# Forget-gate projection units placed between the value projections of a hybrid mixer kernel

## The chip, the cores and the metric

The kernel runs on one core of one Trainium2 chip. The metric is the device time of the program in microseconds (us). The engines are TensorE (PE; its weight loads are listed as PEld), VectorE (DVE), ScalarE (ACT), GpSimd (POOL) and SyncE (SP, which here issues loads); ScalarE also issues DMAs, for the stores.

## The reference, cut to what matters

One layer of a mixer with three kinds of heads over 2048 tokens of width 1024. A modulated RMS norm gives h, one wide projection `p = h @ w_in` is split into thirteen parts, three mixers work on them, and an output projection and a last norm follow.

```
h = rms_norm(x) * (1 + scale) + shift
qa, ka, va, lra, ga, qb, fb, ib, gb, qc, kc, vc, gc = split(h @ w_in)
log_alpha = log_sigmoid(lra @ w_gla_gate2 + b) / 16       # gate of mixer a
log_f = logaddexp(log(lb), log1p(-lb) + log_sigmoid(fb))  # forget gate of mixer b
k_b = (1 - lb) * sigmoid(-fb)
o_a = gated_linear_attn(qa, ka, va, log_alpha)            # 4 heads
o_b = gated_linear_attn(silu(qb), k_b, ib, log_f)         # 4 heads
o_c = stick_breaking_attn(qc, kc, vc)                     # 4 heads
out = rms_norm(x + gate * (concat(gated o_a, o_b, o_c) @ w_out)) * final_norm_w
```

The change concerns the projection to `fb` (256 columns) with the gate's arithmetic behind it, and its place among the projections to `va`, `vc` and `ib`.

## The kernel before, in words

All matmuls of the projections are split in three: high part by high part, high by low, low by high. The split h lies in SBUF as four blocks of 512 tokens (`hT`), taken in the order 3, 2, 1, 0 (`ORDER`).

A unit is one PSUM accumulation. `fm_unit` (lines 149 to 157) gives a 128-column slice of the projection for 512 tokens, columns on partitions, by 24 matmuls of 512 columns; its PSUM tile `acc` comes from `psA`, two buffers. `tm_unit` (159 to 169) gives up to 272 columns for 128 tokens, tokens on partitions, by 24 matmuls of 256 or 272 columns; its PSUM tiles come from `ps1`, four buffers. After each unit an `evac` function takes the result out of PSUM, by a ScalarE copy into a staging tile and a store that ScalarE issues. All staging tiles, of `fm_unit` and of `tm_unit`, have the tag `st` in the pool `stg`, three buffers of 2 KB per partition.

Weights are loaded by `split_w` (135 to 144): SP loads a raw tile (tag `wraw`, two buffers), ScalarE casts the high part (line 141), VectorE subtracts for the low part (line 142). For `fm_unit` they go to the tags `whi` and `wlo` of the pool `wp`, two buffers each; for `tm_unit` to a pool `wv` of its own.

The work around the change, in the order of the text:

- `value_cols` (571 to 575) projects one group of columns for all tokens in 16 `tm_unit`s. It is called for the upper half of `va` with the 16 columns of `lra` (line 629), for `vc` (634), for `ib` (635) and for the lower half of `va` (636).
- The gate of mixer a runs inside the first two of them: `z_units` (599) and `z_out` (609 to 620). `z_out` takes a staging tile `st` and a scratch tile `dz`, which has the tag `whi` or `wlo` of `wp` (line 616).
- Then `st1` is closed, which gives back the value weights, `ps1` and the small tiles, `kp` is opened for the keys and queries of the stick-breaking stream, and the pool `hf` in the same memory behind it.
- The forget gate: two groups of four `fm_unit`s (661 to 664) with `ev_forget` (644 to 659). It copies the PSUM tile to `st` (648), stores it, computes `log_sigmoid` (539 to 544: VectorE, two ScalarE activations, VectorE), `lk = g - st` on GpSimd (653), `bound_decay` (546 to 551: VectorE, two activations, VectorE) and `decay_sums` (523 to 537: a scan and small tiles on VectorE, one activation), stores `bc` to `s_db` (656), computes `lk - bc` on GpSimd (657) and stores it to `s_kb` (658). The tiles `tmp`, `g`, `bc` and `lk` have three buffers each.
- Then the ScalarE table for the sigmoid is loaded (`sig`, line 793), and two streams are interleaved (760 to 777): the stick-breaking attention (`sb_stream`, 680 to 758) and 34 more `fm_unit`s for the features and gates (`fm_stream`, 668 to 678), five of which, the lead units, come first in the text. A step of the stick-breaking stream has two score products (725, 726) into `zt`, a sigmoid (728), a mask on GpSimd (730), a scan of products on VectorE (734), transposes (738), a copy `PT` to SBUF by ScalarE or VectorE (741, 743) and the weighted sums `av` (750). Its loads are `V` and `Dd` (696, 697; combined on VectorE in 698 and 699), `K` (704) and `Q` (709).

The gated linear attention of both mixers, the output projection and the norm follow; they read `s_db`, `s_kb`, `s_ib`, `s_va` and the features back from DRAM.

The order on each engine's queue is fixed when the program is built. Outside the blocks marked as manually ordered, the builder takes what is ready by its own estimate of times, and the text decides between what is ready; so the queues need not follow the text. Tiles take a buffer of their tag when their first instruction is placed.

Of the kernel before, what the change touches and what calls it, by code (L numbers as in the profile page):

```python
# [8 lines left out]
F32 = mybir.dt.float32  # L9
# [9 lines left out]
P = 128  # L19
T = 2048  # L20
# [16 lines left out]
C_QA, C_KA, C_VA, C_LR, C_GA = 0, 256, 512, 1024, 1040  # L37
C_QB, C_FB, C_IB, C_GB = 1552, 1808, 2064, 2320
C_QC, C_KC, C_VC, C_GC = 2576, 2832, 3088, 3344
# [3 lines left out]
def hybrid_mixer_kernel(ctx, tc, x, c, w_ada, b_ada, w_in, w2, bg, gnw, lbl, hnw,  # L43
                        w_out, fnw, masks, sel2, out):
    nc = tc.nc
# [17 lines left out]
    s_vc = dram("s_vc", [T + 1, 256])  # L63
    s_ib = dram("s_ib", [T, 256])
# [124 lines left out]
    def ev_tm(*parts):  # L189
        def f(ps, tt):  # L190
            w = max(b for _, _, b in parts)
            st = stg.tile([P, 272], F32, tag="st", name="stt")
            nc.scalar.copy(st[:, 0:w], ps[:, 0:w])  # L193
            for dst, a, b in parts:
                nc.scalar.dma_start(dst[tt * P:(tt + 1) * P], st[:, a:b])
        return f
# [374 lines left out]
    def value_cols(col0, ncols, step, evac):  # L571
        w = split_w(col0, wv, ncols, step)
        for n in ORDER:
            for u in range(4):
                tm_unit(w, ncols, 4 * n + u, evac)
# [23 lines left out]
    def z_units(n, l4):  # L599
        pt = ps1.tile([96, 512], F32, tag="lr", name="pt", bufs=1)  # L600
        for v in range(4):
            nc.tensor.transpose(pt[:, v * P:(v + 1) * P], l4[:, v, :], ident)
        lrT = vals.tile([96, 512], F32R, tag="lrT", name="lrT")
        nc.vector.tensor_copy(lrT, pt)
        z_ready.extend((n, lrT, j) for j in range(2))
# [16 lines left out]
    def with_z(evac):  # L622
        def f(ps, tt):
            if z_ready:
                z_out(*z_ready.pop(0))
            evac(ps, tt)
        return f

    value_cols(C_VA + 256, 272, 136, with_z(ev_va))
    z_units(*pending.pop(0))  # L630
    vz = vals.tile([1, 256], F32, name="vz")
    nc.vector.memset(vz, 0.0)
    nc.sync.dma_start(s_vc[0:1], vz)
    value_cols(C_VC, 256, 128, with_z(ev_tm((s_vc[1:T + 1], 0, 256))))
    value_cols(C_IB, 256, 128, ev_tm((s_ib, 0, 256)))
    value_cols(C_VA, 256, 128, ev_tm((s_va[:, 0:256], 0, 256)))
    st1.close()

    st2 = ExitStack()
    kp = st2.enter_context(tc.tile_pool(name="kp", bufs=5, reuse_waits="tile"))  # L640
    sth = ExitStack()
    hf = sth.enter_context(tc.tile_pool(name="hf", bufs=3, reuse_waits="tile"))

    def ev_forget(j):
        def f(ps, n):
            nsl = slice(n * 512, (n + 1) * 512)
            st = stg.tile([P, 512], F32, tag="st", name="st")
            nc.scalar.copy(st, ps)
            nc.scalar.dma_start(s_feat["fb"][j][:, nsl], st)
            tmp, g, bc, lk = (hf.tile([P, 512], F32, tag=t, name=t) for t in ("tmp", "g", "bc", "lk"))  # L650
            log_sigmoid(g, st, tmp)

            nc.gpsimd.tensor_tensor(lk, g, st, op=ALU.subtract)
            bound_decay(g, tmp, j)
            decay_sums(2 + j, n, bc, g, 1.0)
            nc.scalar.dma_start(s_feat["db"][j][:, nsl], bc)
            nc.gpsimd.tensor_tensor(lk, lk, bc, op=ALU.subtract)
            nc.scalar.dma_start(s_feat["kb"][j][:, nsl], lk)
        return f

    for j in range(2):
        w = split_w(C_FB + j * P, wp, P, P)
        for n in ORDER:
            fm_unit(w, n, ev_forget(j))
    sth.close()


    def fm_stream(blocks, after):
# [649 lines left out]
```

## Time and profile before

| | |
|---|---|
| time, median of 3 runs | 1297.59 us (1294.85 to 1298.18) |
| the profiled execution's own time | 1294.26 us |
| its span in the trace | 1292.2 us |
| TensorE busy | 1212.9 us, 94% of the span |
| VectorE busy | 742.1 us, 57% |
| ScalarE busy | 471.7 us, 37% |
| GpSimd busy | 162.9 us, 13% |
| mean granted TensorE clock | 0.976 |

The busy time of an engine is the time in which at least one of its instructions runs, so a TensorE that is busy throughout may still be at its lower clock; the granted clock is listed beside it (1.00 is 2.4 GHz, 0.50 is 1.2 GHz). A line of the timeline gives start, duration, engine, source line, operation, output and inputs, and in brackets how long the engine had been idle before and whose instruction released it.

### The profile page before, as it was taken

How to read it: one execution, taken by the hardware profiler on the slowest of the kernel's cores; microseconds unless marked ns; L12 is line 12 of the kernel's file. 1: busy time of each engine (PE TensorE's matmuls, PEld its weight loads, DVE VectorE, ACT ScalarE, POOL GpSimd, SP SyncE). 2: the span in 40 equal slices, each digit the busy share in tenths (PEclk: the TensorE clock that was granted, in tenths of full speed). 3: DMA queues.
4: the chain of work that ended last, by engine and by line, in shares of the span. 5: the costliest groups of instructions: out<-in, count | busy, mean ns of one | idle time of the engine just before them, and what ended most of it. 6: DMA issues, size and time to landing. Idle time of an engine off the chain costs nothing.

```text
span 1292.2 us, 22081 instructions
## 1 busy us (share of the span) xinstructions
PE 1212.9 (94%) x8682; PEld 991.8 (77%) x8682; DVE 742.1 (57%) x1268; ACT 471.7 (37%) x860; POOL 162.9 (13%) x197
## 2 busy tenths in 40 slices
PE   7899999999999789999999999998978897999997
PEld 7777789899998667777777776766867774777775
DVE  4866325700009873535545488877776768765652
ACT  3376423421115342322333244543333434253621
POOL 3210000000003300000000001012432312010000
PEclk8999999999999989999999999998988997999999
DMA  9765442422133341322323323127877657464621
GB/s 265 240 232 180 147 126 91 143 82 86 46 99 112 126 106 54 92 72 86 100 68 86 109 73 92 34 62 238 264 222 208 195 174 241 133 224 132 203 82 51
DMA packets 177566, 173.73 MB, mean 134 GB/s; under 512 B 39625, under 2 KB 131882, under 8 KB 177454
## 3 DMA queue, kind: packets, MB, share of 16 engines
q1 hardware_dynamic: 144970, 128.70, 33.7%
q10 hardware_dynamic: 32484, 43.54, 9.7%
q8 instruction: 70, 1.15, 0.4%
q14 instruction: 42, 0.34, 0.1%
HBM read 113.47 MB, written 58.73 MB: 133 GB/s over the span
## 4 chain that ended last, share of the span: by engine, by line
PE 62%; DVE 13%; DMA 6%; issue 5%; ACT 2%; POOL 1%; SPq 0%; ACTq 0%; POOLq 0%; DVEq 0%
PE av L750 6%; PE acc L154 5%; PE acc L156 5%; PE acc L155 5%; PE acc L166 4%; PE acc L168 4%; PE acc L167 4%; PE pt L738 4%; PE acc L260 4%; PE y L1194 4%; PE y L1192 4%; PE y L1193 4%; DMA kt<-s_kb 2%; DVE W L858 2%; DVE f L734 2%
## 5 line engine op out<-in xcount | busy, mean ns | idle before, releaser
L734 DVE TENSOR_TENSOR_SCAN f<-f 128x512 f32<-128x512 f32 (+3 forms) x160 | 169.9, 1091 | 22.0 <-ACT f L728 11.9
L154 PE MATMUL acc<-hTh,whi 128*128 128x512 f32 x400 | 160.1, 402 | 9.9 <-ACT st L185 4.3
L156 PE MATMUL acc<-hTh,wlo 128*128 128x512 f32 x400 | 157.5, 394 | 0.0
L155 PE MATMUL acc<-hTl,whi 128*128 128x512 f32 x400 | 157.4, 394 | 0.0
L166 PE MATMUL acc<-whi,hTh 128*128 128x256 f32 (+1 forms) x512 | 146.2, 285 | 1.5 <-ACT stt L193 1.5
L168 PE MATMUL acc<-whi,hTl 128*128 128x256 f32 (+1 forms) x512 | 145.8, 285 | 0.0
L167 PE MATMUL acc<-wlo,hTh 128*128 128x256 f32 (+1 forms) x512 | 145.6, 284 | 0.0
L260 PE MATMUL acc<-hTh,whi 128*128 128x512 f32 x240 | 103.8, 432 | 1.7 <-ACT hTh L244 1.7
L260 PE MATMUL acc<-hTl,whi 128*128 128x512 f32 x240 | 97.9, 408 | 4.3 <-DVE hTl L250 4.3
L1192 PE MATMUL y<-wh,hTh 128*128 128x512 f32 x256 | 101.8, 398 | 0.0
L1193 PE MATMUL y<-wl,hTh 128*128 128x512 f32 x256 | 101.6, 397 | 0.0
L728 ACT ACTIVATE f<-zt 128x512 f32<-128x512 f32 (+3 forms) x160 | 82.1, 537 | 52.9 <-DVE f L734 24.7
L1194 PE MATMUL y<-wh,hTl 128*128 128x512 f32 x256 | 100.1, 395 | 0.4 <-DVE hTl L1160 0.4
L166 PEld LDWEIGHTS acc<-whi,hTh 128*128 128x128 f32 x512 | 97.8, 191 | 1.9 <-ACT stt L193 1.7
L154 PEld LDWEIGHTS acc<-hTh,whi 128*128 128x128 f32 x400 | 75.5, 189 | 29.9 <-ACT st L185 5.6
L167 PEld LDWEIGHTS acc<-wlo,hTh 128*128 128x128 f32 x512 | 97.8, 191 | 0.1
L168 PEld LDWEIGHTS acc<-whi,hTl 128*128 128x128 f32 x512 | 97.8, 191 | 0.1
L260 PE MATMUL acc<-hTh,wlo 128*128 128x512 f32 x240 | 97.4, 406 | 0.0
L750 PE MATMUL av<-PT,V 128*64 128x128 f32 x960 | 89.7, 282 | 0.6 <-DVE PT L743 0.6
L156 PEld LDWEIGHTS acc<-hTh,wlo 128*128 128x128 f32 x400 | 75.3, 188 | 17.0 <-issue 1.4
L738 PE MATMUL pt<-ident,f 128*128 128x128 f32 x544 | 87.0, 283 | 0.9 <-DVE f L734 0.7
L155 PEld LDWEIGHTS acc<-hTl,whi 128*128 128x128 f32 x400 | 75.6, 189 | 15.2 <-issue 1.0
(206 smaller groups left out, 2106.8 us busy)
## 6 DMA issues: line engine op xcount, KB each, us to landing
wraw<-in_w_in_dram SPq DMA_DIRECT2D x36, 512.0 KB, 4.9
xt<-in_x_dram SPq DMA_DIRECT2D x16, 512.0 KB, 5.2
wa<-in_w_ada_dram SPq DMA_DIRECT2D x16, 512.0 KB, 5.6
Q<-s_qc SPq DMA_DIRECT2D x64, 128.0 KB, 3.1
ot<-s_o SPq DMA_DIRECT2D x32, 256.0 KB, 3.4
gt<-s_gate SPq DMA_DIRECT2D x32, 256.0 KB, 4.2
r<-in_x_dram SPq DMA_DIRECT2D x16, 512.0 KB, 5.6
out_dram<-r SPq DMA_DIRECT2D x15, 512.0 KB, 2.7
```

The costliest lines, as they stand in the source:

```text
L154: mm(ps, hi[:, k, :], th[:, k, :], start=(k == 0), stop=False)
L155: mm(ps, hi[:, k, :], tl[:, k, :], start=False, stop=False)
L156: mm(ps, lo[:, k, :], th[:, k, :], start=False, stop=(k == KT - 1))
L166: mm(o, th[:, k, s], hi[:, k, 0:ncols], start=(k == 0), stop=False)
L167: mm(o, th[:, k, s], lo[:, k, 0:ncols], start=False, stop=False)
L168: mm(o, tl[:, k, s], hi[:, k, 0:ncols], start=False, stop=(k == KT - 1))
L260: mm(ps, a[:, k, :], b[:, k, :], start=(k == 0 and i == 0), stop=(k == KT - 1 and i == 2))
L734: nc.vector.tensor_tensor_scan(fr, fr, fr, carry[u], op0=ALU.mult, op1=ALU.bypass)
L750: last[0] = mm(av[u * 64:(u + 1) * 64, :], (Dd if diag else V)[J][:, b, :], PT[:, b, :], start=diag, stop=(J == 0 and b == 0))
L1192: mm(y, oh[:, k, us], wh, start=(k == 0), stop=False)
L1193: mm(y, oh[:, k, us], wl, start=False, stop=False)
L1194: mm(y, ol[:, k, us], wh, start=False, stop=(k == KT - 1))
```

## The change

The pool `hf` is opened inside `st1`, with two buffers of `tmp`, `g` and `bc` and one of `lk`. The loop over the two groups of forget units becomes a function `forget_gate(j)`. Group 0 is called between the projections to `vc` and `ib`, group 1 between `ib` and the lower half of `va`. `ev_forget` computes the same. The DMA scratch that is set aside in SBUF at the start of the program is set to 1024 bytes per partition in place of the default, so that all pools fit.

```diff
--- before.py
+++ after.py
@@ -626,20 +626,7 @@
             evac(ps, tt)
         return f
 
-    value_cols(C_VA + 256, 272, 136, with_z(ev_va))
-    z_units(*pending.pop(0))
-    vz = vals.tile([1, 256], F32, name="vz")
-    nc.vector.memset(vz, 0.0)
-    nc.sync.dma_start(s_vc[0:1], vz)
-    value_cols(C_VC, 256, 128, with_z(ev_tm((s_vc[1:T + 1], 0, 256))))
-    value_cols(C_IB, 256, 128, ev_tm((s_ib, 0, 256)))
-    value_cols(C_VA, 256, 128, ev_tm((s_va[:, 0:256], 0, 256)))
-    st1.close()
-
-    st2 = ExitStack()
-    kp = st2.enter_context(tc.tile_pool(name="kp", bufs=5, reuse_waits="tile"))
-    sth = ExitStack()
-    hf = sth.enter_context(tc.tile_pool(name="hf", bufs=3, reuse_waits="tile"))
+    hf = st1.enter_context(tc.tile_pool(name="hf", bufs=2, reuse_waits="tile"))
 
     def ev_forget(j):
         def f(ps, n):
@@ -647,7 +634,8 @@
             st = stg.tile([P, 512], F32, tag="st", name="st")
             nc.scalar.copy(st, ps)
             nc.scalar.dma_start(s_feat["fb"][j][:, nsl], st)
-            tmp, g, bc, lk = (hf.tile([P, 512], F32, tag=t, name=t) for t in ("tmp", "g", "bc", "lk"))
+            tmp, g, bc, lk = (hf.tile([P, 512], F32, tag=t, name=t, bufs=2 - (t == "lk"))
+                              for t in ("tmp", "g", "bc", "lk"))
             log_sigmoid(g, st, tmp)
 
             nc.gpsimd.tensor_tensor(lk, g, st, op=ALU.subtract)
@@ -658,11 +646,25 @@
             nc.scalar.dma_start(s_feat["kb"][j][:, nsl], lk)
         return f
 
-    for j in range(2):
+    def forget_gate(j):
         w = split_w(C_FB + j * P, wp, P, P)
         for n in ORDER:
             fm_unit(w, n, ev_forget(j))
-    sth.close()
+
+    value_cols(C_VA + 256, 272, 136, with_z(ev_va))
+    z_units(*pending.pop(0))
+    vz = vals.tile([1, 256], F32, name="vz")
+    nc.vector.memset(vz, 0.0)
+    nc.sync.dma_start(s_vc[0:1], vz)
+    value_cols(C_VC, 256, 128, with_z(ev_tm((s_vc[1:T + 1], 0, 256))))
+    forget_gate(0)
+    value_cols(C_IB, 256, 128, ev_tm((s_ib, 0, 256)))
+    forget_gate(1)
+    value_cols(C_VA, 256, 128, ev_tm((s_va[:, 0:256], 0, 256)))
+    st1.close()
+
+    st2 = ExitStack()
+    kp = st2.enter_context(tc.tile_pool(name="kp", bufs=5, reuse_waits="tile"))
 
 
     def fm_stream(blocks, after):
@@ -1300,7 +1302,8 @@
     from concourse import mybir as _mybir
     from concourse.bass_utils import run_bass_kernel_spmd as _run
 
-    nc = _bacc.Bacc("TRN2", target_bir_lowering=False, num_devices=1)
+    nc = _bacc.Bacc("TRN2", target_bir_lowering=False, num_devices=1,
+                    dynamic_dma_scratch_size=1024)
     arrays, args = {}, []
     consts = {'masks': _masks(), 'sel2': _selectors()}
     for name in _INS + list(consts):
```

## Rows read from the trace of the kernel before

**Rows 1.** Page, busy time: us, share of the span and instructions of each engine.

```profile
PE 1212.9 (94%) x8682; PEld 991.8 (77%) x8682; DVE 742.1 (57%) x1268; ACT 471.7 (37%) x860; POOL 162.9 (13%) x197
```

**Rows 2.** Windows: length, busy us and instructions per engine, PEclk, DMA share, GB/s.

```profile
260.00:280.00 20.00, 20.00 (x169) 20.00 (x169) 0.00 (x0) 2.61 (x7) 0.00 (x0) 1.00 0.14 47
375.27:450.00 74.73, 67.13 (x287) 53.97 (x286) 59.40 (x95) 30.80 (x53) 25.12 (x16) 0.98 0.37 125
375.27:467.70 92.43, 79.72 (x352) 63.93 (x350) 70.65 (x112) 38.42 (x66) 25.88 (x18) 0.97 0.42 133
440.00:450.00 10.00, 7.49 (x28) 5.73 (x27) 7.92 (x18) 2.15 (x4) 2.59 (x2) 0.83 0.28 105
465.79:482.80 17.01, 17.01 (x120) 12.54 (x120) 14.58 (x16) 6.82 (x15) 0.59 (x2) 0.83 0.11 34
```

**Rows 3.** Timeline of VectorE, its first instruction of the forget gate.

```profile
381.56 0.69 DVE L541 SCALAR_TENSOR_TENSOR tmp<-st 128x512 f32<-128x512 f32 x1 [87.26 <-ACT st L648]
```

**Rows 4.** Timeline of TensorE, three of its six gaps from 375 to 467.

```profile
421.85 0.50 PE L154 MATMUL acc<-hTh,whi 128*128 128x512 f32 x1 [2.33 <-ACT st L648]
...
444.80 0.79 PE L154 MATMUL acc<-hTh,whi 128*128 128x512 f32 x1 [2.51 <-ACT st L185]
...
465.79 0.69 PE L750 MATMUL av<-PT,Dd 128*64 128x128 f32 x4 [4.38 <-DVE PT L743]
```

**Rows 5.** Timeline of ScalarE: copies of the last value units and first forget units.

```profile
372.59 0.37 ACT L193 COPY stt<-acc 128x256 f32<-128x256 f32 x1 [2.51 <-PE acc L168]
373.00 0.33 ACTq L195 DMA_DIRECT2D s_va<-stt  x1
375.47 0.37 ACT L193 COPY stt<-acc 128x256 f32<-128x256 f32 x1 [2.51 <-PE acc L168]
...
380.94 0.59 ACT L648 COPY st<-acc 128x512 f32<-128x512 f32 x1 [5.09 <-PE acc L156]
...
386.38 0.59 ACT L648 COPY st<-acc 128x512 f32<-128x512 f32 x1 [2.71 <-PE acc L156]
```

**Rows 6.** Waits of the SP queue, 150 to 480: us in total, times, longest.

```profile
SPq L696 <- DMA s_db<-bc: 17.5, 1, 17.5
```

**Rows 7.** Timeline of VectorE at the sixth gap.

```profile
464.65 0.48 DVE L698 SCALAR_TENSOR_TENSOR Dd<-V,nm,Dd 128x256 f32<-128x256 f32 x1 [3.49 <-DMA Dd<-s_vc]
```

**Rows 8.** Timeline of GpSimd and of ScalarE's queue, the first forget unit.

```profile
384.48 1.29 POOL L653 TENSOR_TENSOR lk<-g,st 128x512 f32<-128x512 f32 x1 [170.37 <-DVE g L544]
...
395.99 0.33 ACTq L658 DMA_DIRECT2D s_kb<-lk  x1
```

**Rows 9.** DMA issues, 175 to 480: count, KB each, median us to landing.

```profile
s_ib<-stt ACTq DMA_DIRECT2D x16, 128.0 KB, 1.7
...
s_kb<-lk ACTq DMA_DIRECT2D x8, 256.0 KB, 3.0
```

**Rows 10.** Chain of waits, 225 to 470: start us, us, what.

```profile
246.76 4.13 DMA s_vc<-stt
```

**Rows 11.** Timeline of TensorE, the two gaps in the value projections.

```profile
246.42 0.50 PE L611 MATMUL pz<-lrT,w 96*128 96x512 f32 x1 [1.43 <-ACT st L613]
...
251.34 0.38 PE L166 MATMUL acc<-whi,hTh 128*128 128x256 f32 x1 [1.53 <-ACT stt L193]
```

**Rows 12.** Timeline of TensorE: an early score product, and the next feature unit.

```profile
451.74 0.39 PE L725 MATMUL zt<-K,Q 128*128 128x512 f32 x1
...
482.79 0.47 PE L154 MATMUL acc<-hTh,whi 128*128 128x512 f32 x1
```

**Rows 13.** Timeline of VectorE, the first three scans of the stick-breaking stream.

```profile
453.97 2.21 DVE L734 TENSOR_TENSOR_SCAN f<-f 128x384 f32<-128x384 f32 x2 [0.19 <-POOL f L730]
...
458.07 1.28 DVE L734 TENSOR_TENSOR_SCAN f<-f 128x512 f32<-128x512 f32 x1
```

**Rows 14.** Timelines of ScalarE and VectorE: last cast for vc, last z_out.

```profile
170.52 1.05 ACT L141 CAST whi<-wraw 128x1024 fp32r<-128x1024 f32 x1 [1.92 <-DMA wraw<-in_w_in_dram]
...
248.50 0.69 DVE L541 SCALAR_TENSOR_TENSOR dz<-st 128x512 f32<-128x512 f32 x1 [1.40 <-ACT st L613]
```

## The prediction

> **What bounds the kernel now.** I read the page first. TensorE is busy for 94% of the span [rows 1], so the time can only fall where TensorE stands idle or runs at its lower clock. Then I cut the span into windows around the edit, to see which stretch has either. In a plain value stretch TensorE is busy for 20.00 of 20.00 us at clock 1.00, while VectorE has no instruction at all (first line of [rows 2]). In the stretch from the first forget matmul to the first weighted sum of the stick-breaking stream, 375.27 to 467.70, TensorE is busy for 79.72 of 92.43 us: 12.7 us idle (third line of [rows 2]). So work that needs VectorE stands in one place, and right ahead of it VectorE does nothing for 87.26 us [rows 3].
>
> TensorE's timeline says what ends the idle time. There are six gaps. Five, 8.3 us together (2.33 the first, 2.51 the longest), end with a ScalarE copy out of PSUM, of a forget unit or of a lead unit queued behind one; the sixth, 4.38 us, ends with the copy PT of the stick-breaking stream [rows 4]. The cause of the five is VectorE: 59.40 us of work up to 450 for eight units (second line of [rows 2]), 7.4 us each, against 5.44 us that TensorE needs for a unit (distance of two copies, [rows 5]). The sixth has another cause. The loads of V were held 17.5 us on SP until a forget tile had been stored, since they reuse its memory [rows 6]; the last loads then landed late, and VectorE, in order, stood 3.49 us at Dd before it reached PT [rows 7].
>
> The lower clock (1.2 GHz in place of 2.4 in part of a window) costs too: the mean is 0.83 over 7.49 busy us and 0.83 over 17.01 (lines 4 and 5 of [rows 2]), so 0.17 x 24.5 = 4.2 us of full-speed work. Idle and clock together, 16.9 us are the most that the edit can give back here.
>
> **The change, part by part.** *Nothing is removed.* Eight units of 24 matmuls move ahead: four before the projection at C_IB, four before the one at C_VA. Their ScalarE, VectorE and GpSimd work moves along, and so do two weight loads on SP and 24 stores on ScalarE's queue. 8 x 5.44 = 43.5 us of TensorE are spent earlier, the first group by 92 us and the second by 46, so the last value unit, which ended at 375.3, ends at 418.8.
>
> *Cover.* A value unit takes 2.88 us [rows 5], 16 of them 46.1 us. Each group of four forget units brings 4 x 7.4 = 29.7 us of VectorE work; its own TensorE time (21.8) and the value units behind it (46.1) give 67.9 us of cover. The five gaps (8.3 us) go. If the value units did not cover, VectorE would set 7.4 us for a unit and the gaps would be back.
>
> *Fewer buffers.* tmp, g and bc have 2 in place of 3, lk has 1. With a single lk, a unit's first lk instruction waits until the previous unit's kb store has landed: 384.48 to 395.99 plus 3.0 us [rows 8, 9], 14.5 us per unit. Four take 58 us, under the 67.9 of cover, so this chain alone costs nothing; above 17 us per round it would run into the next group. But the staging tile st of a forget unit is held until that lk instruction, and the value units' stt come from the same three buffers. The first lk instruction ends some 10 us into a group, so st of the third unit is held until 10 + 2 x 14.5 = 39 us and of the fourth until 53; between 22 us, where the group's matmuls end, and 39 us (about six value units) one buffer serves the value units. One use of it takes 0.41 us from copy to issue [rows 5] and the landing, 1.7 us [rows 9]: 2.1, under 2.88, no stall. The long end is a landing of 4.13 us, seen on the chain of waits just where gate stores and value stores met [rows 10]: 4.5, which loses 1.7 us per unit. TensorE lost 1.43 + 1.53 = 2.96 us there [rows 11]. I take 0 and 2.96 us per group as the ends, and the middle, 3.0 us for both, since both groups do mix such stores but the four PSUM buffers of value units absorb about three units.
>
> *Weights and queues.* The two forget weight loads pass in front of the value weights on SP. VectorE, which splits weights, is free in the value stretch, so I cost that at nothing; its cover is the 46 us of value units, and without it a split (cast 1.05 us, [rows 14]) would stand in the open. The smaller DMA scratch only makes room; the stores and loads around the edit are issued from ScalarE and SP [rows 6, 9], so nothing: 0 both ways.
>
> *The start of the stick-breaking stream.* PSUM of the value units frees at 418.8, and five lead units (5 x 5.44 = 27.2 us) follow, to 446.0. Under them V, Dd, K and Q load and the sigmoid table loads, so the 4.38 us gap goes. What stays is the ramp. Before, the first three scans ran early, under the lead units; the six steps that follow took 17.01 us (last line of [rows 2]), to 482.79, where the next feature unit starts [rows 12]. With TensorE always supplied, I expect the queue order (fixed at build) to place the first scores behind the lead units. Then 2.2 us from score to scan (451.74 to 453.97, [rows 12, 13]; it may be less, as the table load stood there before) and three scans, 2.21 + 1.28 = 3.5 us [rows 13], come in the open: 446.0 + 2.2 + 3.5 + 17.0 = 468.7, in place of 482.79. Gain 14.1 us; 2.8 of the 16.9 stay behind as ramp.
>
> *The clock, row and rule.* The window with the 2.51 us gap has 0.83, and the one behind the 4.38 us gap 0.83 again [rows 2, 4], while the value stretch without a gap has 1.00 (first line of [rows 2]); my sum leaves the six steps as long as they were, at their lower clock, so it returns only the first 1.3 us of the 4.2 for certain. The Trainium skill (TensorE: Matmul & The Clock Gate, section HAM oscillation) says that the clock drops through gaps in which TensorE waits and that the loss is half of the throttled time. By that rule the whole 4.2 us would return, and the gain would be 16.9 - 3.0 = 13.9 us.
>
> **Sum.** -14.1 + 3.0 = -11.1 us. Against the profiled execution's 1294.26 us: 1283.2. The median shown, 1297.59, stands 3.3 us above that execution, so in medians 1286.5. Behind 482.79 the work is the same in the same amounts, and TensorE is what the page shows as full, so I carry the gain along to the end.
>
> **Rivals.** *A, everything comes back.* Scores and scans of the stream slip under the lead units as they did before, and no staging stall appears: -16.9, median 1281. For it: scores did run between feature units before, as at 451.74 [rows 12]. Against it: they did so because TensorE was waiting.
>
> *B, the gain is mostly eaten.* Either the queue order keeps the forget units together, or both stalls are at their long end (5.9 us) and the new order of the stream, which is settled again from the first step on, loses about 5 us: -14.1 + 5.9 + 5 = -3 us, median 1294, from -7 to 0. For it: a delay such as the 3.49 us at Dd comes from queue order alone. Against it: nothing forces such a loss.
>
> *C, slower, through the weight buffers.* The scratch of the gate units z_out and the forget weights take turns in the same two whi and wlo buffers. The forget raw load now follows the one split at 170.52, so its weights may hold a buffer from then on, while the last z_out came as late as 248.50 [rows 14]; if the second forget weights take the other one, the last two z_out wait for the first group to end, and hold two of the three staging buffers. It decides when a value store then lands in 4.13 and not in 1.7 us: twelve value units lose 1.7 each, 20 less the 8.6 us that PSUM absorbs, 11.4; some 5 us more for the first group's own copies, and 2.96 for the second: 19.4 against 14.1, +5.3 us, median 1303. Against it: 1.7 us is the landing of most value stores. The Trainium skill (Perfetto Trace Analysis, section Optimization Strategy) also speaks against the change: consistent bubbles can mean that there is too little memory for the next tile, and this edit takes buffers away. No row here shows such a bubble in a value stretch beyond the two gaps of [rows 11].
>
> **Chances.** Forecast 0.50, A 0.20, B 0.18, C 0.12. A measurement of this kernel tells 0.3% (3.9 us) from no change. Faster: 0.50 + 0.20 + a third of B = 0.76; same: the rest of B, 0.12; slower: C, 0.12. The range reaches from A, with about 1 us of spread, 1280, to the end of B, 1298, and leaves out C and the edges.
>
> **What would show it.** Right: TensorE at 20.00 of 20.00 through all value and forget units; VectorE busy there; no ScalarE copy ending a TensorE gap before the lead units; no wait of SP for db before V; the first feature unit behind the stream's start near 469. Wrong: gaps at the value matmuls ended by the copy stt (staging, B or C), z_out ending after the first forget group (C), a gap over 4 us at the first scores, or a later end of the stream than the gain explains.

## The result, and the profile after

The changed kernel takes 1281.3 us (median of four runs, 1281.14 to 1283.09) against 1297.6 us for the kernel before (four runs, 1294.85 to 1298.18): a ratio of 0.9879, interval 0.9864 to 0.9894, a gain of 16.3 us. Forecast were 1286.5 us and a gain of 11.1. The profiled execution of the changed kernel took 1281.43 us, span 1279.7.

The line of busy time on the page (columns as in [rows 1]) shows that TensorE does the same work in less span:

```profile
PE 1211.2 (95%) x8682; PEld 990.4 (77%) x8682; DVE 729.3 (57%) x1268; ACT 471.4 (37%) x860; POOL 160.5 (13%) x197
```

In the changed kernel the line numbers of the edited part shift: the forget gate's copy is L635, its `lk` L641 and L645, the scores L727 and L728, the scan L736, `PT` L743 and L745, `av` L752, the loads of V L698, of Q L711. The windows, columns as in [rows 2]; the first is the whole value stage with both forget groups in it, 350 to 374 lies in the second group, 418.90 to 446.70 holds the lead units, 446.70 to 466.43 is the stretch from there to the next feature unit, and 300 to 350 lies in the first group and the value units behind it:

```profile
183.00:418.90 235.90, 234.33 (x1751) 225.60 (x1750) 96.23 (x243) 75.79 (x153) 23.27 (x18) 1.00 0.30 100
...
350.00:374.00 24.00, 24.00 (x117) 20.24 (x116) 8.04 (x15) 8.86 (x15) 3.93 (x3) 1.00 0.17 62
418.90:446.70 27.80, 27.80 (x125) 23.07 (x124) 6.94 (x12) 5.38 (x8) 0.29 (x1) 1.00 0.65 175
440.00:460.00 20.00, 19.20 (x113) 13.95 (x111) 12.16 (x13) 8.23 (x17) 1.18 (x4) 1.00 0.26 80
446.70:466.43 19.73, 18.93 (x140) 13.11 (x139) 17.11 (x18) 10.35 (x22) 0.88 (x3) 1.00 0.14 43
...
300.00:350.00 50.00, 50.00 (x399) 49.14 (x398) 17.68 (x37) 14.66 (x32) 10.45 (x7) 1.00 0.30 103
```

The value stage now holds VectorE's work, 96.23 us, and TensorE is idle in it for 1.57 us; under the lead units it is never idle, and between them and the next feature unit for 0.80 us. The clock is 1.00 in every line, where the kernel before had 0.83 twice [rows 2].

TensorE's timeline of the changed kernel: the five gaps over 0.15 us that are left between 236 and 490, two score products inside the lead units, the next feature unit, and the last product of the stick-breaking stream:

```profile
246.66 0.50 PE L611 MATMUL pz<-lrT,w 96*128 96x512 f32 x1 [0.54 <-ACT st L613]
...
250.38 0.50 PE L154 MATMUL acc<-hTh,whi 128*128 128x512 f32 x1 [0.33 <-ACT whi L141]
...
252.30 0.39 PE L166 MATMUL acc<-whi,hTh 128*128 128x256 f32 x1 [0.70 <-ACT stt L193]
...
440.70 0.33 PE L727 MATMUL zt<-K,Q 128*128 128x384 f32 x1
...
452.40 0.44 PE L752 MATMUL av<-PT,Dd 128*64 128x128 f32 x4 [0.32 <-DVE PT L745]
...
456.52 1.09 PE L752 MATMUL av<-PT,V 128*64 128x128 f32 x14 [0.33 <-DVE PT L745]
...
466.43 0.47 PE L154 MATMUL acc<-hTh,whi 128*128 128x512 f32 x1
...
854.03 0.38 PE L752 MATMUL av<-PT,V 128*64 128x128 f32 x2
```

Beside [rows 4, 11]: the gaps over 0.15 us between 236 and 490 sum to 2.22 us, and to 15.66 in the kernel before, 13.4 less. The 4.2 us of low clock are gone too. Against that the value units begin 1.2 us later (182.7, before 181.5), and variants of the changed kernel, below, begin between 181.0 and 183.5, one at 188.5; what sets this was not found. So 13.4 + 4.2 - 1.2 = 16.4 us is what the two executions should differ by at the next feature unit; they do by 482.79 [rows 12] - 466.43 = 16.36. At the stream's last product it is 15.4 us (854.1, before 869.5). Nothing more is won behind it. (The second pair of profiles, below, agrees less closely.)

### The profile page after: what moved, and what is told of

Its sections match the earlier page's. It is cut to its first block, busy times and chain, and to the rows that moved or that the text cites. A ratio compares the mean times of both kernels' runs of the same rounds, so it can differ in the third digit from the quotient of the medians.

```text
span 1279.7 us, 22082 instructions
## 1 busy us (share of the span) xinstructions
PE 1211.2 (95%) x8682; PEld 990.4 (77%) x8682; DVE 729.3 (57%) x1268; ACT 471.4 (37%) x860; POOL 160.5 (13%) x197
## 4 chain that ended last, share of the span: by engine, by line
PE 64%; DVE 8%; issue 7%; DMA 7%; ACT 2%; POOL 1%; SPq 0%; ACTq 0%; POOLq 0%; DVEq 0%
PE acc L154 6%; PE acc L156 6%; PE acc L155 6%; PE av L752 6%; PE acc L260 5%; PE pt L740 4%; PE y L1195 4%; PE y L1196 4%; PE y L1194 4%; PE acc L166 4%; PE acc L168 4%; PE acc L167 4%; PE zt L727 2%; PE zt L728 2%; DVE f L736 2%
## 5 line engine op out<-in xcount | busy, mean ns | idle before, releaser
L736 DVE TENSOR_TENSOR_SCAN f<-f 128x512 f32<-128x512 f32 (+3 forms) x160 | 169.7, 1090 | 29.3 <-POOL f L732 14.5
L752 PE MATMUL av<-PT,V 128*64 128x128 f32 x960 | 88.8, 280 | 0.7 <-DVE PT L745 0.7
L860 DVE SCALAR_TENSOR_TENSOR W<-W,SX,U 64x128 f32<-64x128 f32 (+1 forms) x248 | 77.7, 313 | 16.5 <-PE U L849 6.9
```

The source lines that it names most:

```text
L736: nc.vector.tensor_tensor_scan(fr, fr, fr, carry[u], op0=ALU.mult, op1=ALU.bypass)
L752: last[0] = mm(av[u * 64:(u + 1) * 64, :], (Dd if diag else V)[J][:, b, :], PT[:, b, :], start=diag, stop=(J == 0 and b == 0))
```

## The experiments

The theory: TensorE waited since VectorE's 7.4 us for a forget unit had only 5.44 us of TensorE work beside it, and since the loads of V and Dd waited for the forget tiles' memory; the new place gives the first enough cover and puts the second out of the way. The rivals: only the memory counts (the smaller pools and scratch free V early), or the number of buffers and the order of the queues decide and the cover is incidental. Two things were not run: the small DMA scratch by itself, and more staging buffers in the order of before. Each group of kernels ran beside the kernel before on the same chip; its medians were 1298.13, 1298.16 and 1299.36 us. This table gives, for each profiled execution, when the first value unit starts, when the last matmul of the last one starts, and when the stream's last product does, in us of the trace, and then the time of the runs and its ratio to the kernel before:

| kernel | value units | last product | median us | ratio, interval |
|---|---|---|---|---|
| before, again | 181.4 to 375.5 | 869.6 | 1298.15 | 0.9996 (0.9983 to 1.0008) |
| after, again | 183.1 to 419.4 | 853.6 | 1281.51 | 0.9876 (0.9852 to 0.99) |
| one group moved | 182.8 to 397.1 | 855.6 | 1285.34 | 0.9915 (0.9892 to 0.9939) |
| before, other memory | 181.3 to 375.8 | 864.5 | 1295.5 | 0.9971 (0.9955 to 0.9988) |
| after, single buffers | 182.7 to 418.6 | 852.8 | 1283.24 | 0.9889 (0.9866 to 0.9912) |
| before, less VectorE work | 181.4 to 375.5 | 857.6 | 1287.13 | 0.9929 (0.9906 to 0.9951) |
| after, both groups in one place | 183.4 to 439.2 | 870.3 | 1298.27 | 0.9997 (0.9984 to 1.001) |
| after, four staging buffers | 188.5 to 423.0 | 857.4 | 1285.06 | 0.9894 (0.9877 to 0.9912) |
| after, more VectorE work | 181.7 to 418.0 | 852.8 | 1284.82 | 0.9892 (0.9865 to 0.9919) |
| before, more VectorE work | 182.1 to 375.8 | 884.6 | 1314.43 | 1.0113 (1.0084 to 1.0143) |
| after, no lead units | 183.5 to 419.9 | 866.6 | 1295.77 | 0.9969 (0.9956 to 0.9983) |
| after, feature units spread further | 181.0 to 417.0 | 853.2 | 1287.38 | 0.991 (0.9887 to 0.9933) |

### Both kernels again

No edit to either.

> The kernel before once more, for a second profile. Ratio 1.000. What is open: its profiled execution was 3.3 us under its median. The profiles so far differ most between the first score product of the gated linear attention and its last state update: 174.5 us in the profile of before, 175.5 and 180.0 in two profiles of the changed kernel, 177.7 to 181.5 in three others. If that stage varies from execution to execution, this profile shows the value and forget stages as the first did (the six gaps within 0.5 us, the first feature unit at 483 within 1 us, the last weighted sum at 869 to 870), and the attention stage at 176 to 182 us. If the rows behind the prediction were peculiar to one execution, the gaps differ.

> The changed kernel once more, for a second profile and a tighter interval. Both theories: about 1281 us, 16 us under the kernel before. What is open: in the first pair of profiles the changed kernel is 16.4 us ahead at the first feature unit behind the start of the stick-breaking stream (482.79 to 466.43) but only 12.8 us at the end. If the 3.6 us given back belong to the program, this profile shows them again in the output stage and the runs give about -13; if they are the profiled execution of the kernel before, which was 3.3 us under its median, the runs give about -16.

The gain is there again, 16.6 us. In these two profiles the streams end 16.0 us apart, in the first two 15.4.

The second profile of the kernel before does not repeat all gaps within the 0.5 us that were expected. TensorE's second gap among the forget units, in the first profile and in the second:

```profile
429.74 0.50 PE L154 MATMUL acc<-hTh,whi 128*128 128x512 f32 x1 [1.71 <-ACT st L648]
```

```profile
430.05 0.50 PE L154 MATMUL acc<-hTh,whi 128*128 128x512 f32 x1 [0.21 <-ACT st L648]
```

The unit starts equally long after the one ahead of it (7.89 us from 421.85 [rows 4], 7.88 us from 422.17): in the second profile the lower clock fell behind the first gap (0.83 between 420 and 430), so the matmuls took the time that was idle time in the first. In the same way one gap of 1.95 us stands in the value projections in place of the two of [rows 11]. The gaps sum to 12.8 us and not 15.7, and the low clock makes some 6 to 7 us and not 4.2. So where a copy decides when the next unit starts, low clock takes the place of idle time and costs nothing more; only the two together can be compared between executions. The first feature unit behind the start of the stream comes at 481.93, 1.1 us off the 483 that was expected within 1, and this pair is 14.9 us apart there, not 16.4.

### One group moved

Group 0 stays between `vc` and `ib`; group 1 goes back behind the last value units, with three buffers for each of its tiles:

```diff
     value_cols(C_IB, 256, 128, ev_tm((s_ib, 0, 256)))
-    forget_gate(1)
     value_cols(C_VA, 256, 128, ev_tm((s_va[:, 0:256], 0, 256)))
...
+    sth = ExitStack()
+    hf[:] = [sth.enter_context(tc.tile_pool(name="hfb", bufs=3, reuse_waits="tile")), None]
+    forget_gate(1)
+    sth.close()
```

> Only group 0 of the forget units moved, group 1 behind the last value projection with three buffers as before. Theory (uncovered VectorE work, and V loads held by forget tiles): behind the last value unit stand 4 x 7.4 = 30 us of VectorE work against 9 x 5.44 = 49 us of TensorE work (four forget units, five lead units), so at most some 3 us of gaps stay, and the V loads are free before the lead units end: 13 to 16 us under the kernel before, 1282 to 1285. Rival (each moved unit brings its own share): half of 16, 8 us under it, about 1290.

Measured: 1285.34 us, 12.8 less than the kernel before, just short of the 13 to 16 expected. TensorE's timeline has one gap over 1 us left:

```profile
443.09 0.50 PE L154 MATMUL acc<-hTh,whi 128*128 128x512 f32 x1 [1.32 <-ACT st L185]
```

Its gaps over 0.15 us from 236 to 490 sum to 4.18 us. So four of the eight units bring most of the gain: the 29.7 us of VectorE work of the other four find their cover in their own 21.8 us of matmuls and in the lead units behind. The shortage of the kernel before arises only when eight come in a row, and the gain is not proportional to what is moved.

### The kernel before with other memory for the forget tiles

The order of the kernel before; the forget tiles lie at the other end of SBUF, so that V and Dd do not reuse their memory, and the DMA scratch is the small one:

```diff
-    hf = sth.enter_context(tc.tile_pool(name="hf", bufs=3, reuse_waits="tile"))
+    hf = sth.enter_context(tc.tile_pool(name="hf", bufs=3, side="right", reuse_waits="tile"))
```

> The order of before, with the forget tiles (three buffers) in memory of their own on the other side of SBUF, so that V and Dd need not wait for them. Theory: the five gaps that end with ScalarE copies stay (8.3 us), the 4.38 us gap and the low clock behind it (2.9 us at most) go: 4 to 7 us under the kernel before, about 1291 to 1293, and no wait of SP for the db store before V. Rival (it is all VectorE behind the units, and the loads are hidden anyway): no change, 1297.

Measured: 1295.5 us, 2.6 less. TensorE's timeline at what was the sixth gap, and the windows there:

```profile
463.98 0.44 PE L750 MATMUL av<-PT,Dd 128*64 128x128 f32 x4 [0.67 <-DVE PT L743]
```

```profile
440.00:460.00 20.00, 16.33 (x65) 12.57 (x64) 15.32 (x28) 7.82 (x13) 4.07 (x5) 0.91 0.58 169
460.00:480.00 20.00, 19.33 (x145) 14.58 (x144) 18.63 (x24) 9.51 (x19) 1.13 (x2) 1.00 0.26 73
```

The gap of 4.38 us [rows 4] is 0.67, and the clock behind it is 1.00. Four of the five gaps that end with ScalarE copies are still there (up to 2.52 us, beside 2.51 before), and with them 0.91 between 440 and 460. At the stream's last product the kernel is 5.0 us ahead. One expectation failed: SP still waits for forget stores ahead of V and Dd, as its waits show:

```profile
SPq L697 <- DMA s_db<-bc: 7.7, 2, 5.2
SPq L696 <- DMA s_db<-bc: 5.2, 1, 5.2
```

The first load of V is issued at 438.95, 11.8 us earlier than the 450.79 of the kernel before, but not at once; what else holds it there stays open. So the loads that came late were behind the sixth gap, and other memory for the forget tiles (with the small scratch) is worth some 5 us of the stream, less in the runs (2.6 us by the medians, 1.6 to 5.8 by the interval). The rival that memory is all falls.

### The kernel before with less VectorE work, and both kernels with more

Less: in the order of the kernel before, `log_sigmoid` and `bound_decay` keep their four activations but lose three of four VectorE steps, and the clamp behind the scan goes. More: in both kernels the scan of each forget unit is done four times over, 8 x 3 scans of 1.23 us, 29.5 us of VectorE work. The core of the two edits:

```diff
-            log_sigmoid(g, st, tmp)
+            nc.scalar.activation(tmp, st, AF.Exp, scale=-0.01)
+            nc.scalar.activation(tmp, tmp, AF.Ln, bias=one_col)
+            nc.scalar.activation(tmp, tmp, AF.Exp, scale=-1.0)
+            nc.scalar.activation(tmp, tmp, AF.Ln, bias=one_col)
+            nc.vector.scalar_tensor_tensor(g, st, 0.0, tmp, op0=ALU.min, op1=ALU.subtract)
...
-            bound_decay(g, tmp, j)
-            decay_sums(2 + j, n, bc, g, 1.0)
+            decay_sums(2 + j, n, bc, g, 1.0, False)
```

```diff
-        nc.vector.tensor_tensor_scan(bc, rmask, g, 0.0, op0=ALU.mult, op1=ALU.add)
+        for _ in range(1 + more):
+            nc.vector.tensor_tensor_scan(bc, rmask, g, 0.0, op0=ALU.mult, op1=ALU.add)
```

> The order of before, with less VectorE work in the forget gate: the first step of log_sigmoid, both VectorE steps of bound_decay and the clamp are left out; the four ScalarE activations stay, so the decay values are others. VectorE has 7.4 - 0.82 - 0.54 - 0.69 - 0.43 = 4.9 us for a unit, under TensorE's 5.44. Theory (VectorE sets the pace of the five gaps): they go (8.3 to under 2 us), the forget tiles are free earlier, and so V: 10 to 16 us under the kernel before, 1282 to 1288, without a unit moved. Rival (the pace is set by ScalarE's queue, with its copies behind activations and store issues, or by the lk tile's round): the gaps stay at 5 us or more, 1292 or more.

> The kernel before with the same three scans more in each forget unit. Theory (there the chain stands in the open): VectorE has 8 x 11.1 = 89 us for the eight units where TensorE has 13 x 5.44 = 71, so nearly all of the 29 us are seen: 20 to 29 us over the kernel before, 1318 to 1327. Rival (the gaps come from the order of ScalarE's queue, VectorE has slack): under 10 us, 1308 or less.

> The changed kernel with the scan of each forget unit done four times in place of once (the same values), 3 x 1.2 = 3.7 us more VectorE work on the chain of each unit, 29 us in all. Theory (the chain runs under the value units, up to a round of 17 us): the lk round grows from 13 to 16.7 us, still covered: 0 to 3 us over the changed kernel, 1281 to 1285. Rival (there is no slack left, the staging tiles are held too long): 10 us or more over it, gaps at copies stt.

Less work: 1287.13 us, 11.0 less than the kernel before by the medians (6 to 12 by the interval of the ratio), with nothing moved. Of the six gaps these two are left, 3.2 us:

```profile
426.65 0.50 PE L154 MATMUL acc<-hTh,whi 128*128 128x512 f32 x1 [0.97 <-ACT st L649]
...
434.65 0.50 PE L154 MATMUL acc<-hTh,whi 128*128 128x512 f32 x1 [2.27 <-ACT st L185]
```

That is more than was expected to stay, and why these two stay was not followed up; but the sixth gap is gone as well: VectorE, free earlier, lets the forget tiles go earlier, and the first load of V is issued at 440.82 in place of 450.79.

More work, in the place of before: 1314.43 us, 15.1 above the kernel before on that chip, and the stream's last product is 15 us later; less than the 20 to 29 us expected. TensorE's two longest gaps:

```profile
455.12 0.80 PE L154 MATMUL acc<-hTh,whi 128*128 128x512 f32 x1 [4.66 <-ACT st L185]
...
476.37 0.79 PE L726 MATMUL zt<-K,Q 128*128 128x512 f32 x1 [6.94 <-DMA s_kb<-lk]
```

About half of the extra work is taken up by what lies beside it; the rest stands in the open. More work, in the new place: 1284.82 us, with a ratio that cannot be told from that of the changed kernel (the intervals cover each other), and the last product at 852.8, not later. Its window, to be laid beside the last window of the changed kernel above, and GpSimd's `lk` of the first group:

```profile
300.00:350.00 50.00, 50.00 (x402) 49.26 (x401) 28.93 (x44) 13.94 (x29) 7.79 (x6) 1.00 0.26 90
```

```profile
292.10 1.30 POOL L642 TENSOR_TENSOR lk<-g,st 128x512 f32<-128x512 f32 x1 [77.88 <-DVE g L545]
...
310.01 1.30 POOL L642 TENSOR_TENSOR lk<-g,st 128x512 f32<-128x512 f32 x1 [3.02 <-DMA s_kb<-lk]
...
326.24 1.30 POOL L642 TENSOR_TENSOR lk<-g,st 128x512 f32<-128x512 f32 x1 [2.65 <-DMA s_kb<-lk]
...
341.36 1.29 POOL L642 TENSOR_TENSOR lk<-g,st 128x512 f32<-128x512 f32 x1 [2.66 <-DMA s_kb<-lk]
```

VectorE is busy for 28.93 us of 50 in place of 17.68, a round takes up to 17.9 us, and TensorE is busy for 50.00 of 50.00 in both. Over the whole value stage, to be laid beside the first window of the changed kernel above, VectorE's work grows from 96.23 to 122.81 us, and TensorE's idle time from 1.57 to 1.85:

```profile
183.00:418.00 235.00, 233.15 (x1742) 224.43 (x1741) 122.81 (x262) 74.66 (x150) 20.65 (x17) 1.00 0.29 97
```

The same 29.5 us cost 15 us in the one place and nothing that shows in the stage in the other: this is the cover, seen directly.

### Single buffers

In the changed kernel all four forget tiles have one buffer:

```diff
-            tmp, g, bc, lk = (hf.tile([P, 512], F32, tag=t, name=t, bufs=2 - (t == "lk"))
+            tmp, g, bc, lk = (hf.tile([P, 512], F32, tag=t, name=t, bufs=1)
```

> The changed kernel with one buffer of each forget tile (tmp, g, bc, lk) in place of 2, 2, 2, 1. Theory (value units cover the chain, and the lk round of 13 us already sets its pace): the round stays under the 17 us that a quarter of a forget group with its value stage gives, TensorE has no gap: within 2 us of the changed kernel, 1281. Rival (the fewer buffers are what the change pays with): the staging buffers are held longer, TensorE waits at value units with copies stt as releasers: 4 us or more over the changed kernel, 1285 or more.

Measured: 1283.24 us, with an interval that overlaps that of the changed kernel; gaps of 2.01 us in all. Buffers of these tiles are not what limits. The Trainium skill (Perfetto Trace Analysis, section Optimization Strategy) lets one ask for memory when bubbles repeat: here the repeated bubbles of the kernel before [rows 4], in which each tile had three buffers, went away with fewer of these tiles in the new place. Whether more staging buffers would have closed them in the old place was not run.

### Both groups in one place

```diff
     forget_gate(0)
-    value_cols(C_IB, 256, 128, ev_tm((s_ib, 0, 256)))
     forget_gate(1)
+    value_cols(C_IB, 256, 128, ev_tm((s_ib, 0, 256)))
```

> Both groups of forget units between the projections to vc and ib, one behind the other. Theory (value units cover the chain, wherever they stand): eight lk rounds of 13 us are 104 us; 8 x 5.44 + 32 x 2.88 = 136 us of TensorE work stand beside and behind them, so no new gap: within 2 us of the changed kernel, 1280 to 1284. Rival (the split in two groups, each with value units behind it, is what makes it work): the later forget units wait for staging and PSUM buffers, 43.5 us of matmuls against 104 us of chain, gaps at copies st of 4 us or more, 1286 or more.

Measured: 1298.27 us: the whole gain is gone, which the theory of cover, put so simply, did not expect, since 32 value units stand behind the eight. TensorE's timeline, ScalarE's from 318 on, and the windows:

```profile
344.17 0.50 PE L154 MATMUL acc<-hTh,whi 128*128 128x512 f32 x1 [1.91 <-ACT st L635]
...
355.94 0.58 PE L166 MATMUL acc<-whi,hTh 128*128 128x256 f32 x1 [4.43 <-ACT stt L193]
...
464.11 0.68 PE L740 MATMUL pt<-ident,f 128*128 128x128 f32 x3 [3.80 <-DVE f L736]
```

```profile
318.79 0.59 ACT L635 COPY st<-acc 128x512 f32<-128x512 f32 x1 [5.95 <-POOL lk L641]
...
343.53 0.58 ACT L635 COPY st<-acc 128x512 f32<-128x512 f32 x1 [6.21 <-POOL lk L641]
...
355.51 0.37 ACT L193 COPY stt<-acc 128x256 f32<-128x256 f32 x1 [5.87 <-POOL lk L641]
```

```profile
340.00:375.00 35.00, 28.66 (x170) 26.16 (x170) 15.88 (x31) 11.10 (x23) 7.31 (x6) 0.85 0.22 80
460.00:480.00 20.00, 15.84 (x114) 11.60 (x113) 16.24 (x19) 7.48 (x16) 0.58 (x2) 0.91 0.20 63
```

Two things are to be seen. ScalarE's copies wait 5.95, 6.21 and 5.87 us for `lk` on GpSimd, and with it for a staging tile: the forget units' `st` that the prediction feared to be held too long are held, once eight units follow each other, and behind the second and third of these waits TensorE is idle for 6.3 us between 340 and 375, at a clock of 0.85; the first leaves none (40.00 of 40.00 us busy from 300 to 340). And the built queue of TensorE has two of the five lead units inside the value stage; only 72 feature matmuls, three units, stand behind the last value unit (its last matmul starts at 439.2), and the first scan of the stream stands in the open (3.80 us), behind a VectorE that is idle for 11.21 us until a load of `Dd` lands. So the loss has two parts: the staging tiles, and loads that have three units of cover and not five. For the first, cover has to come by the portion: four units with 16 value units behind them are within what three staging tiles and the PSUM buffers carry, eight are not.

### Four staging buffers

In the changed kernel `stg` has four buffers, paid for with single buffers of the forget tiles (edit of the single buffers, and):

```diff
-        stg = stA.enter_context(tc.tile_pool(name="stg", bufs=3))
+        stg = stA.enter_context(tc.tile_pool(name="stg", bufs=4))
```

> The changed kernel with one buffer of each forget tile, and the memory that this frees used for a fourth staging buffer. Theory: the only gaps left in the value stage, 0.54 + 0.33 + 0.70 us near 250, end with copies that wait for a staging buffer, so they go: at most 1.6 us under the changed kernel, 1279 to 1281. Rival: those gaps come from the order of ScalarE's queue, no change, 1281 to 1283.

Measured: 1285.06 us, not the 1279 to 1281 expected. From the first value unit to the stream's first weighted sum it takes 268.1 us, and the changed kernel 269.7: the gain that was looked for. But the value units begin 5.8 us later (188.5), in a stage ahead of all that the edit was meant for, and that is more than it wins. What delays the first stage was not followed up, and the intervals of the two ratios overlap.

### No lead units

The number of feature units placed ahead of the stream goes from five to none:

```diff
-               34, sig.ins, marks, 5)
+               34, sig.ins, marks, 0)
```

> The changed kernel with no lead units: the feature units are interleaved with the stick-breaking stream from its first step on. Theory (the start of the stream costs nothing because five units of 5.44 us stand between the last value unit, which frees its memory, and the first scores): loads of V, Dd and Q (3 to 4 us), sigmoid table, first scans come in the open; a gap of 3 to 6 us at the first scores and low clock behind it, 3 to 8 us over the changed kernel at the first steps. Rival (the ramp is hidden by the feature units wherever they stand): no gap over 1 us there, within 2 us of the changed kernel.

Measured: 1295.77 us, and the last product 13 us later than in the changed kernel (866.6), more than expected. TensorE's timeline, and SP's issues (the view ends at 431):

```profile
433.62 0.66 PE L727 MATMUL zt<-K,Q 128*128 128x384 f32 x1 [8.00 <-DMA Q<-s_qc]
```

```profile
420.07 0.37 SPq L698 DMA_DIRECT2D V<-s_vc  x1
...
424.46 5.02 SPq L706 DMA_DIRECT2D K<-s_kc  x8
429.52 1.93 SPq L711 DMA_DIRECT2D Q<-s_qc  x3
```

V waits until the last value unit has run; its tiles lie in memory that the value weights had. Then 18 loads, up to the second of the two for the first Q, are issued one behind the other from 420.07 to 430.80, about 0.6 us each, and the first scores wait for Q. One feature unit runs in that time, and TensorE stands for the rest, 8.00 us. The lead units are the cover of just this.

### Feature units spread further

The changed kernel with the feature units laid out over 52 steps of the stream, not 40 (`80 // 2` becomes `52` in the call of `interleave`).

> The changed kernel with the feature units spread over 52 of the 80 steps of the stick-breaking stream in place of 40. From 720 to 860 us VectorE limits the stream and TensorE idles 5.4 us in both kernels, since the feature units have run out. Theory: more of them there fill these gaps, 0 to 4 us under the changed kernel, 1277 to 1281. Rival: the feature units that end later hold back the memory, and with it the loads, of the attention behind the stream: the same or slower, 1281 or more.

Measured: 1287.38 us, by the ratios some 4 us slower than the changed kernel, with intervals that just overlap. TensorE's idle time from 720 to the end of the stream is 4.8 us, beside 6.5 and 5.5 in the two profiles of the changed kernel, but the stream ends no earlier (853.2). Whether the rival's memory is the reason was not tested. No kernel of this study has a lower median than the changed one.

## Why the prediction was right or wrong

**Right: what bounds, and that it comes back.** The two causes were told apart as [rows 2 to 7] suggested, and each has its run: VectorE's work (15 us for 29.5 us more of it in the old place, some 9 to 11 us back for less of it, nothing that shows in the new place) and the late loads of V (5 us of the stream with other memory alone). That a forget tile's memory is all that held V, as the prediction read [rows 6], is only half borne out: with other memory SP still waited, though V was issued 11.8 us earlier. V waits elsewhere now, as SP's waits in the changed kernel show (us in total, times, longest):

```profile
SPq L698 <- DMA s_va<-stt: 29.7, 1, 29.7
SPq L698 <- PE acc L168: 13.0, 1, 13.0
```

It waits until the value stage is over: the first load of V is issued at 418.98, and the loads run under the lead units.

**Right: cover, rounds and the value stage.** The last value unit was put at 418.8; the first lead unit starts at 418.91. That this is so close is in part luck: the value units began 1.2 us later, and the old gaps of [rows 11] shrank by 1.4. A round of the single `lk` was put at 14.5 us; it takes 13.2, 13.1 and 11.3 in the first group (12.3, 13.7 and 11.3 in the second), by GpSimd's timeline of the changed kernel:

```profile
292.86 1.29 POOL L641 TENSOR_TENSOR lk<-g,st 128x512 f32<-128x512 f32 x1 [77.62 <-DVE g L544]
...
306.07 2.35 POOL L641 TENSOR_TENSOR lk<-g,st 128x512 f32<-128x512 f32 x1 [2.54 <-ACT whi L141]
...
319.21 1.30 POOL L641 TENSOR_TENSOR lk<-g,st 128x512 f32<-128x512 f32 x1 [2.63 <-DMA s_kb<-lk]
...
330.53 1.30 POOL L641 TENSOR_TENSOR lk<-g,st 128x512 f32<-128x512 f32 x1 [2.64 <-DMA s_kb<-lk]
```

In two of the three brackets the releaser is the `kb` store, as the argument had it.

**Wrong by 3.0 us: the staging stall.** The step took the middle of 0 and 2.96 us for each group; measured are 0. ScalarE did wait, as its waits between 183 and 470 show:

```profile
ACT stt L193 <- DMA s_ib<-stt: 5.8, 3, 2.7
ACT stt L193 <- DMA s_va<-stt: 4.5, 2, 2.7
...
ACT stt L193 <- DVE bc L537: 3.3, 2, 1.6
...
ACT stt L193 <- DVE fl L1087: 3.1, 1, 3.1
ACT stt L193 <- POOL lk L645: 2.8, 1, 2.8
ACT stt L193 <- POOL lk L641: 2.0, 1, 2.0
```

That is 21.5 us in ten waits, none over 3.1, and between 252.3 and 452.0 TensorE has no gap over 0.15 us: the PSUM buffers carried each one. Four of the ten, 9.2 us, are of a kind that the prediction did not have: `bc` and the second `lk` are awaited by stores ahead of the copy in ScalarE's queue, not by a staging tile. The prediction had named the cushion and still put in half of the long end. It has an end: with eight units in a row the waits were 5.95, 6.21 and 5.87 us, and at the last two TensorE stood. The old gaps of the value stage went from 2.96 us [rows 11] to 1.57; the builder put half of the first forget unit (12 matmuls) beside them, at 250 and 255. In the second pair of profiles they are 1.95 and 1.82, so this cannot be called a gain.

**Wrong by some 2.3 us: the clock at the start of the stream.** From the end of the lead units to the next feature unit the step allowed 22.7 us (446.0 to 468.7): 5.7 for score to scan and three scans, and 17.0 for the six steps, as long as before at their lower clock. The 5.7 us came out as put: from 446.70 to the first weighted sum at 452.40 it is 5.70 us, and TensorE, with score products and transposes to do, is idle for 0.46 of it. The six steps are what was mis-sized: 14.03 us (452.40 to 466.43) in place of 17.0. They hold the same transposes and weighted sums as before and four score products fewer, and their clock is 1.00, where the kernel before had 0.83; so of the 4.2 us of low clock not 1.3 but all returned. Against that the lead units end 0.7 us later than put, half of it the two score products that the built order places among them (440.70): 2.97 - 0.7 = 2.3. The 2.8 us that the sum left behind as ramp were thus the clock of the six steps. That it all returns is the outcome by the rule of the Trainium skill (TensorE: Matmul & The Clock Gate, section HAM oscillation) that the prediction had set beside its sum; the trace agrees with it here, since with no gap over 1.44 us left between 140 and 860 every window of 20 us there has 1.00, while the experiment with a gap of 4.43 us has 0.85 around it. The two terms together, 3.0 + 2.3 = 5.3 us, are the difference between 482.79 - 466.43 = 16.4 and the 11.1 forecast; by the second pair, 14.9 us apart, it would be 3.8.

**The rivals.** *A* (-16.9, 1281 us) has the number that was measured, and half of its mechanism: no staging stall appeared. Its other half, scores and scans that slip under the lead units as before, came only in part: one pair of scores and one scan stand there (440.70), and the other scores and scans stand behind, as the forecast had it. What brought its number is the clock, which it counted as returned in full. *B* did not come: in both built programs the order of TensorE, VectorE, ScalarE and GpSimd from the next feature unit to the stream's last product is the same (2524 matmuls on TensorE), so there was no new order to lose by. Its first branch, units kept together, is real all the same: the run with both groups in one place is that case. *C* did not come, as ScalarE's timeline of the changed kernel shows:

```profile
259.61 0.33 ACTq L620 DMA_DIRECT2D s_da<-dz  x1
260.71 1.05 ACT L141 CAST whi<-wraw 128x1024 fp32r<-128x1024 f32 x1 [1.77 <-DMA s_da<-dz]
```

The second cast of forget weights is released by a store of the gate's scratch: the weights waited for the last `z_out`, not the other way round.

**The sum against the profiled time.** Carrying the gain to the end held only roughly: 15.4 us at the stream's last product became 12.8 in the times of the two profiled executions, and 16.3 in the medians. The last section says why.

## What to carry to other kernels

Where an engine beside TensorE has more work in a unit than TensorE, put such units between others that leave it idle, in portions that the buffers in between can carry; one lump of the same size gave nothing here, in part for that reason. Count a wait of the copying engine as lost only beyond what the PSUM buffers hold, and read the clock in the windows around each gap, since closing the gaps here also returned the low clock behind them (4.2 us). Compare idle time and low clock between executions only as a sum. What a freed wait uncovers next (here loads that wait for the value weights) needs its own cover, and the lead units that gave it were worth 12 to 13 us.

## What was not expected of the hardware

Stages that the edit does not touch differ between executions of one program by more than the edit's smaller terms. The gated linear attention, from its first scores to its last state update, took 174.5 us in one execution of the kernel before and 178.5 in another, and 175.5 and 180.0 in two of the changed kernel. At the stream's last product the two executions of the kernel before are within 0.2 us of each other (869.5 and 869.6), at their end 5.8 us apart, and 4.0 of these arise in that stage. So the profiled execution of before lay 3.3 us under its median mostly for a reason far behind the edit, and a difference of two profiles should be taken at the end of the stage in question, not at the end of the span. What makes that stage vary was not tested.
